# Regenerating a one-core hybrid decoder in the order its own list schedule found, with PSUM banks dealt again in eleven rounds

## The chip, the cores and the metric

The kernel runs on one core of a Trainium2 chip, as one launch. The metric is the device time of one execution in microseconds (us). The time before is the median of three runs.

## The reference, cut to what matters

One layer of a decoder trunk over 4096 tokens of width 1024: a norm, one wide input projection, two groups of recurrent heads that read it, an output projection with a residual add, and a last norm.

```python
h = _rmsnorm(x, norm_w)
u = (h @ w_in).astype(f32)
...
q_in = qc * jnp.exp(b)                    # gated linear attention, 4 heads, in chunks
k_in = kc * jnp.exp(-b)
...
def step(S, inp):                          # RWKV-7, 8 heads of 64, one token after another
    r_t, w_t, k_t, v_t, kk_t, a_t = inp
    sa = jnp.einsum('bhvk,bhk->bhv', S, -kk_t)
    S = (S * w_t[:, :, None, :]
         + sa[..., None] * (kk_t * a_t)[:, :, None, :]
         + v_t[..., None] * k_t[:, :, None, :])
    y = jnp.einsum('bhvk,bhk->bhv', S, r_t)
    return S, y
...
merged = jnp.concatenate([gla_out, rwkv_out], axis=-1).astype(x.dtype)
return x + merged @ w_out
```

## The kernel before

**Tiling.** The tokens are cut into 8 blocks of 512. A weight or an activation is held as two fp16 halves, so a projection of 128 columns is 3 x 8 pairs of matmuls with 512 moving columns. A pair is two matmuls of 64 columns each that run beside each other in the array (`duo`, L497, whose inner matmul stands on L509; all other instructions stand on L457, where the recording engine puts them). A block has 17 projections for the RWKV group (tiles `wr`), 12 for the attention group (`wg`; four of them, the values, are written with the operands exchanged and stand as `bank<-wg,x` with 128 moving columns, 384 matmuls for each two), and 8 for the output (`wo`).

**The recurrence.** A unit is a pair of RWKV heads of a block, so there are 32 units, numbered 0 to 31. `rwkv_ab` (L899) makes its operands: after the projections of key and receptance DVE writes `DD` and `bk`, PE multiplies them (`bank<-DD,bk`, 16 matmuls), and the masked product `Nb` has to be inverted. The inversion goes through DRAM (`nd`, then the tile `f`), runs as 62 small dependent steps on POOL (tiles `Tc`, `tm`; on DVE for unit 31 alone), goes back through DRAM (`td`), and ends in `rwkv_i` (L1049) with `bank<-Ta,Nb` and `bank<-Nb,Ta` on PE. `rwkv_c` (L1071) then runs the chain of 8 chunks: `ch<-sv,DD` on PE, a copy `us` on ACT, `ch<-us,Nb` on PE, a copy `uv` on ACT, `ch<-uv,bk` on PE, and the new state `sv` on DVE, three matmul steps for a chunk, each waiting for the one ahead of it. The chains of the units follow each other, since the state tile of a head pair goes from block to block. `rwkv_d` (L1114) normalises the outcome (`bank<-crs,bones`).

**The end.** `out_last` (L1339) makes the last block's output in two parts: the six mixing tiles that are ready early (`bank<-x,wo`), and then the tiles of units 30 and 31 (`bank<-x,x`, 96 matmuls), a norm and the stores.

**The start.** `stream_w` (L1463) reads, scales and splits all 37 weight tiles during the first block, on ACT and DVE.

**What sets the order.** Nothing is issued as the Python runs. Generators (`stream_x` to `stream_o`, and the chains) are advanced by `run` (L477), which keeps a rough clock with `account` (L183) and takes the ready generator of least priority. Each operation is recorded by `put` (L240) as a `Step` with its engine, a modelled duration, and the steps it must follow, found from the regions of tiles that it reads and writes (`parts`, L117; `whole`, L217). Some decisions are taken in this recording and never again: which of the six PSUM banks (`bank0` to `bank5`) a result gets (`need`, L789, takes the one that the rough clock says is free first), and so which earlier reader it has to wait for. Columns of small tables (`TABLES`, L100: scales, packed parameters, carries) are no regions for `parts`; `whole` lists them, and a step that shares only such a column with an earlier one follows its start, without a duration.

Then a list schedule is made. `forward` (L281) places the steps in time on six engines with a priority for each; `backward` (L349) makes the next priorities from the end times. Ten passes of both are made from the first order for each of five settings (`keep`, the bonus for staying in the same shape of array, and `look`, how far ahead an engine waits for a better step), the order with the smallest modelled end is kept, and the instructions are written in order of their modelled start times:

```python
first_order = forward([s.t0 for s in steps])
best = first_order
for keep, look in ((0.5, 0.15), (0.5, 0.3), (0.7, 0.3), (1.0, 0.15), (2.0, 0.3)):
    start, end = first_order
    for _ in range(10):
        start, end = forward(backward(end), keep, look)
        best = min(best, (start, end), key=lambda x: max(x[1]))
```

Every engine and the one DMA queue, SP's, then works through its instructions in that order.

Of the kernel before, what the change touches and what calls it, by code (L numbers as in the profile page):

```python
# [20 lines left out]
P = 128  # L21
DM = 1024
# [24 lines left out]
NC = TB // C  # L47
GUP = 2.0 ** 19
# [33 lines left out]
def hymba_kernel(ctx, tc, xT, wt, wg, wo, wua, gup, pk, ck, out):  # L82
# [16 lines left out]
    TABLES = ("pkt", "scl", "invs", "hinv", "mu_s", "omu_s", "carry", "wosc", "woinv", "gnh", "lnh")  # L99
    FINE = {"Nb": 32, "f": 16}  # L100
    HEADS, XS = set(), set()
    now = [0.0]
    streams = []
    ready, used, busy = {}, {}, {}

    def dram(ap):

        name = ap.tensor.name
        if name.startswith("nd"):
            return [(name, i) for i in (range(4) if ap.shape[0] == 32 and len(ap.shape) == 2 else [ap.offset // (NC * 1024) % 4])]  # L110
        if name.startswith("td"):
            return [(name, i) for i in (range(4) if ap.ap[0][0] >= 1024 else [ap.offset // 1024 % 4])]
        if name.startswith("wdr"):
            return [(name, i) for i in ([ap.offset // (P * DM) % 2] if ap.ap[0][1] == P and len(ap.shape) == 3 and ap.shape[1] == KT and ap.shape[2] == P else range(2))]
        return [(name, 0)]

    def parts(ap):  # L117
        if ap.tensor.name == out.tensor.name or ap.tensor.name.rsplit("_", 1)[0] in TABLES:
            return []
        if ap.space == DRAM:  # L120
            return dram(ap)
        a = ap.start_partition()
        tag = ap.tensor.name.rsplit("_", 1)[0].rstrip("0123456789_")
        if tag in FINE:
            q = FINE[tag]
            return [(ap.tensor.name, h) for h in range(a // q, (a + ap.shape[0] - 1) // q + 1)]
        hs = range(a // 64, (a + ap.shape[0] - 1) // 64 + 1)
        if ap.tensor.name in HEADS:
            o = ap.offset % P // 64
            e = range(2) if ap.ap[-1][1] > 64 else range(o, o + 1)  # L130
            return [(ap.tensor.name, h, i) for h in hs for i in e]
        if ap.tensor.name in XS:
            o = ap.offset % (4 * TB) // TB
            e = range(o, o + max(1, math.prod(ap.shape[1:]) // TB)) if ap.dtype == F16 else range(4)
            return [(ap.tensor.name, h, 2 + i) for h in hs for i in e]
        return [(ap.tensor.name, h) for h in hs]

    def place(eng, t, d):

        q = busy.setdefault(eng, [])  # L140
        while q and q[0][1] < now[0] - 100:
            q.pop(0)
        i = 0
        for i, (a, e) in enumerate(q):
            if t + d <= a:
                break
            t = max(t, e)
        else:
            i = len(q)
        q.insert(i, (t, t + d))  # L150
        return t

    class Array:


        def __init__(self):
            self.tile, self.form, self.f32, self.free, self.clock = {}, None, False, 0.0, [0, 0.0, True]

        def put(self, t, d, cols, tiles):
            r, c, f32 = tiles[:3]  # L160
            form = (r[1] - r[0], c[1] - c[0]) + tuple(tiles[3:])
            q = [(i, j) for i in range(r[0], r[1]) for j in range(c[0], c[1])]
            turn = form != self.form
            t = max([t, self.free] + [self.tile.get(k, 0.0) for k in (self.tile if turn else q)]) + 0.09 * turn
            w, k = int(t / 3.413), self.clock
            if w > k[0]:
                k[:] = [w, 0.0, w == k[0] + 1 and k[1] >= 3060]
            k[1] += cols
            d *= 1 if k[2] else 2
            full = len(q) == 16  # L170
            if full and f32 == 2:
                d += 0.005
            elif f32 and form == (2, 4):
                d += 0.008
            for k in q:
                self.tile[k] = t + (d if full or not f32 else 0.66 * d)
            self.form, self.f32 = form, f32 > 0
            self.free = t + (d if full or turn and f32 else d / 2 if f32 and form != (4, 1) else 0.014)
            return t, d

    array = Array()

    def account(eng, out, ins, d, lag, cols=0, tiles=None):  # L183
        rdy = lambda k: (lambda r: r[0] + early(r[1], eng))(ready.get(k, (0.0, "")))
        t = max([0.0] + [rdy(k) for a in ins for k in parts(a)]
                + [used.get(k, 0.0) for k in parts(out)]
                + [rdy(k) for k in parts(out) if eng != "T"])
        if eng == "T":
            t0, d = array.put(max(t, now[0]), d, cols, tiles)
            t, now[0] = t0, array.free  # L190
        else:
            if eng == "D":
                t0 = place("H", t, 0.5)
                t = t0 + 1.15
            t = place(eng, t, d)
            if eng != "D":
                t0 = t
        for a in ins:
            for k in parts(a):
                used[k] = max(used.get(k, 0.0), t + d + (0.95 if eng == "D" else 0.1))  # L200
        for k in parts(out):
            ready[k] = (t + d + lag, eng)
        return t0

    def early(a, b):

        if a not in "VSGT" or b not in "VSGT" or not a:
            return 0.0
        if a == b:
            return {"V": -0.075, "S": -0.1, "G": -0.18, "T": 0.0}[a]  # L210
        return -0.045 if a == "T" else 0.0 if b == "T" else -0.04

    table = [0]
    steps, wkey, rkey, wlast, readers = [], {}, {}, {}, {}
    last, turn, lead = [None, 0], [0], []

    def whole(ap):  # L217
        if ap.tensor.name == out.tensor.name:
            return []
        if ap.space == DRAM:  # L220
            return dram(ap)
        if ap.tensor.name.rsplit("_", 1)[0] in TABLES:
            w = math.prod(ap.tensor.shape[1:])
            return [(ap.tensor.name, i) for i in range(ap.offset % w, ap.offset % w + math.prod(ap.shape[1:]))]
        return parts(ap)

    class Step:


        def __init__(self, n, t0, eng, d, lag, cols, tiles, tab, f, both=False):  # L230
            self.n, self.t0, self.eng, self.d, self.lag, self.f, self.both = n, t0, eng, d, lag, f, both
            self.cols, self.tiles, self.tab, self.on, self.to, self.next = cols, tiles, tab, {}, [], None
            self.form = tiles and (tiles[0][1] - tiles[0][0], tiles[1][1] - tiles[1][0]) + tuple(tiles[3:])
# [6 lines left out]
    def put(t0, eng, d, lag, cols, tiles, tab, outs, ins, f):  # L240
# [3 lines left out]
        for k in list(ki) + list(ko):  # L244
            t0 = max(t0, wkey.get(k, 0.0))
# [1372 lines left out]
```

## Time and profile before

| | |
|---|---|
| median of three runs | 2261.45 us (2260.09 to 2263.47) |
| the profiled execution, own time | 2259.63 us |
| its span, first to last instruction | 2257.9 us |
| granted clock of TensorE, mean | 0.985 |
| DVE busy | 1706.8 us, 76% |
| ACT busy | 1249.7 us, 55% |
| POOL busy | 874.7 us, 39% |

A row of a timeline gives the start and the length in us, the engine, the line, the operation, what is written and read, the shape, the type and the count, and in brackets the idle time of the engine ahead of it with what ended it. PEld is the loading of weights on PE. A float32 matmul stands as two in the trace. In a table of windows the columns are the stretch, its length, the busy time and the number of instructions of PE, PEld, DVE, ACT and POOL, the granted clock of TensorE, the share of the DMA engines and their rate.

### The profile page before, as it was taken

The numbers are of one execution on the slowest core, as the hardware profiler recorded it, in microseconds if no ns is written. First come the engines' busy times: TensorE is split into PE (matmuls) and PEld (weight loads), VectorE is DVE, ScalarE is ACT, GpSimd is POOL, SyncE is SP. The second block draws the span as 40 slices with busy tenths as digits, with TensorE's granted clock in tenths as the row PEclk, the third lists the DMA queues.
The fourth block names the chain that finished last, engine by engine and source line by source line (L and its number), as shares of the span: only waits on it lengthen the run. The fifth ranks groups of instructions, "written<-read, shape, count | busy, mean of one in ns | idle before, by whom it ended". The sixth has DMA issues, their size and how long they took to land.

```text
span 2257.9 us, 75272 instructions
## 1 busy us (share of the span) xinstructions
PE 2154.3 (95%) x30800; PEld 1377.6 (61%) x30800; DVE 1706.8 (76%) x3801; ACT 1249.7 (55%) x3229; POOL 874.7 (39%) x2212
## 2 busy tenths in 40 slices
PE   7899999989999999999999999999999999999986
PEld 3656665556755567556675666655675565756653
DVE  7989788488783887768776886847878578776866
ACT  7677674455554646545554547445565555545442
POOL 2551334425344342436525154342624444262400
PEclk9999999999999999999999999999999999999988
DMA  6786554465344553456434553445534455344432
GB/s 193 223 262 207 166 181 146 114 194 145 88 127 127 185 149 94 116 150 202 120 103 126 179 156 110 116 129 178 156 92 123 140 179 149 100 118 137 146 86 80
DMA packets 275455, 326.91 MB, mean 145 GB/s; under 512 B 131572, under 2 KB 132772, under 8 KB 275108
## 3 DMA queue, kind: packets, MB, share of 16 engines
q1 hardware_dynamic: 275108, 322.10, 48.7%
q8 instruction: 241, 3.95, 0.7%
q14 instruction: 106, 0.87, 0.1%
HBM read 276.94 MB, written 45.05 MB: 143 GB/s over the span
## 4 chain that ended last, share of the span: by engine, by line
PE 63%; DVE 21%; DMA 8%; ACT 3%; issue 3%; SPq 1%; POOL 0%; DVEq 0%; ACTq 0%; POOLq 0%
PE bank L509 50%; PE bank L457 8%; PE ch L509 4%; DMA xr<-in_xT_dram 3%; DVE DD L457 3%; DVE nta L457 2%; DVE bk L457 2%; PE y L457 1%; DVE x L457 1%; SPq L457 1%; DVE xr L457 1%; DVE sv L457 1%; DVE Nb L457 1%; PE y L509 1%; DVE mgr L457 1%
## 5 line engine op out<-in xcount | busy, mean ns | idle before, releaser
L509 PE MATMUL bank<-x,wr 128*64 128x512 f16 x6528 | 795.5, 381 | 10.4 <-DVE DD L457 5.4
L457 POOL TENSOR_TENSOR tm<-Tc,f 128x60 f32<-128x60 f32 (+24 forms) x961 | 350.0, 364 | 667.7 <-DMA f<-nd 585.4
L509 PEld LDWEIGHTS <-wr 128*64 128x64 f16 x6528 | 361.1, 110 | 265.0 <-issue 27.2
L457 POOL TENSOR_TENSOR Tc<-Tc,tm 128x60 f32<-128x60 f32 (+24 forms) x961 | 357.3, 372 | 74.4
L509 PE MATMUL bank<-x,wg 128*64 128x512 f16 x3072 | 373.1, 384 | 3.8 <-ACT ta L457 2.2
L509 PE MATMUL bank<-x,wo 128*64 128x512 f16 x2976 | 360.9, 383 | 3.4 <-DVE DD L457 2.8
L457 POOL TENSOR_TENSOR xacc<-xacc,xr 128x512 f32<-128x512 f32 x98 | 129.7, 1324 | 364.0 <-ACT xr L457 235.2
L509 PEld LDWEIGHTS <-wg 128*64 128x64 f16 x3072 | 172.3, 111 | 130.5 <-issue 9.9
L457 DVE SCALAR_TENSOR_TENSOR sv<-ch,PC,psd 64x64 f32<-64x64 f32 x448 | 126.3, 282 | 143.3 <-PE ch L509 129.6
L509 PEld LDWEIGHTS <-wo 128*64 128x64 f16 x2976 | 162.8, 111 | 115.9 <-issue 9.2
L509 PEld LDWEIGHTS <-x 128*64 128x64 f16 x6240 | 190.8, 111 | 30.1 <-issue 20.0
L509 PE MATMUL bank<-wg,x 128*64 128x128 f16 x6144 | 194.8, 220 | 11.4 <-DMA wg<-wdr 7.2
L457 ACT ACTIVATE psd<-sv,PC 128x128 f32<-128x128 f32 x256 | 102.3, 400 | 165.3 <-DVE sv L457 143.0
L457 ACT COPY us<-ch 64x64 f32<-64x64 f32 x512 | 104.7, 205 | 94.5 <-PE ch L509 86.4
L457 ACT COPY uv<-ch 64x64 f32<-64x64 f32 x512 | 105.0, 205 | 93.9 <-PE ch L509 88.6
L457 ACT ACTIVATE sa<-bank,mu_s 128x512 f32<-128x512 f32 x104 | 71.5, 688 | 73.2 <-PE bank L509 69.9
L457 DVE COPY_PREDICATED Nb<-mc,bank 64x512 f32<-64x512 uint8 x128 | 92.8, 727 | 8.4 <-PE bank L457 6.4
L509 PEld LDWEIGHTS ch<-us,Nb 128*64 128x64 f32 x1024 | 68.5, 138 | 48.5 <-ACT us L457 15.3
L509 PEld LDWEIGHTS ch<-uv,bk 128*64 128x64 f32 x1024 | 68.0, 139 | 47.5 <-ACT uv L457 12.8
L509 PEld LDWEIGHTS ch<-sv,DD 128*64 128x64 f32 x1024 | 67.0, 138 | 46.7 <-DVE sv L457 14.4
L457 DVE COPY_PREDICATED DD<-mc,bank 64x512 f32<-64x512 uint8 x128 | 93.4, 731 | 2.3
L457 PE MATMUL bank<-DD,bk 64*128 64x128 f32 x1024 | 77.7, 286 | 11.4 <-DVE bk L457 7.4
(333 smaller groups left out, 3559.8 us busy)
## 6 DMA issues: line engine op xcount, KB each, us to landing
wr<-wdr SPq DMA_DIRECT2D x256, 256.0 KB
wg<-wdr SPq DMA_DIRECT2D x184, 256.0 KB
xr<-in_xT_dram SPq DMA_DIRECT2D x176, 256.0 KB
wo<-wdr SPq DMA_DIRECT2D x128, 256.0 KB
f<-nd SPq DMA_DIRECT2D x128, 128.0 KB
x<-in_wt_dram SPq DMA_DIRECT2D x29, 512.0 KB
wdr<-wo SPq DMA_DIRECT2D x25, 512.0 KB
out_dram<-mgg SPq DMA_DIRECT2D x33, 256.0 KB
```

The lines of the kernel that those rows point to most:

```text
L457: put(t0, self.name, d, lag, cols, tiles, tab, outs, ins, lambda: f(*a, **kw))
L509: nc.tensor.matmul(x, lhsT=l, rhs=y, start=start, stop=stop)
```

## The change

The recording is wrapped into a function `build(guide)`, and everything in it moves one level to the right. It is called eleven times. The first time `guide` is empty and the recording goes as before. In each later round `guide` holds, for every step of the round ahead (by the name of its generator and its number in it), the start and the end that the list schedule gave it:

- `run` advances the generator whose next step is due first by `guide`, in place of the one of least priority.
- `need` sorts the banks by the time at which they are left by `guide`, and if the bank it would take is left more than 1 us after the asking generator's next step is due, it puts the generator off once until then.
- `put` takes the start in `guide` as the step's first rank.

In each round there are five passes of `forward` and `backward` with one setting, `keep` 1.0 and `look` 0.15; the round with the smallest modelled end of the eleven is the one that is written out. Tiles are made once and shared by the rounds (`store`). Columns of tables become regions of `parts`; `whole` goes, and all dependencies carry their latency. The diff is shown without the changes of indentation and cut to its core; `forward`, `backward`, `account`'s body and the streams are as they were.

```diff
+LOOKS = ((1.0, 0.15),)
+PASSES = 5
+PUT_OFF = 1.0
+ROUNDS = (LOOKS,) * 11
...
+    store = {}
+    ident = one.tile([P, P], F32, tag="ident_0", name="ident_0")
+    make_identity(nc, ident)
+
+    def build(guide):
...
+        cur, nth, leave = ["init"], {}, {}
+        due = lambda who: guide.get((who, nth.get(who, 0)), (-1.0, -1.0))
...
-        if ap.tensor.name == out.tensor.name or ap.tensor.name.rsplit("_", 1)[0] in TABLES:
+            if ap.tensor.name == out.tensor.name:
             return []
...
+            if tag in TABLES:
+                w = math.prod(ap.tensor.shape[1:])
+                return [(ap.tensor.name, i) for i in range(ap.offset % w, ap.offset % w + math.prod(ap.shape[1:]))]
...
-        keys = lambda aps: {k: k in {y for x in aps for y in parts(x)} for a in aps for k in whole(a)}
+            keys = lambda aps: dict.fromkeys(k for a in aps for k in parts(a))
...
+            key = (cur[0], nth.get(cur[0], 0))
+            nth[cur[0]] = key[1] + 1
+            if key in guide:
+                t0 = guide[key][0]
+                for a in outs + ins:
+                    if a.space == PSUM:
+                        leave[a.tensor.name] = max(leave.get(a.tensor.name, 0.0), guide[key][1])
...
             can = [s for s in streams if s[2] is None or s[2]()]
+                if guide:
+                    s = min(can, key=lambda s: max(s[1], due(s[4])[0]))
+                else:
...
-            banks.sort(key=bank_free)
-            if len(banks) >= n and bank_free(banks[n - 1]) <= now[0]:
+                banks.sort(key=(lambda t: leave.get(t.tensor.name, 0.0)) if guide else bank_free)
+                if len(banks) >= n and (guide or bank_free(banks[n - 1]) <= now[0]):
+                    t = leave.get(banks[n - 1].tensor.name, 0.0)
+                    if guide and not put_off and t > due(cur[0])[0] + PUT_OFF:
+                        put_off = True
+                        yield (t,)
+                        continue
                 break
...
+        guide, best = {}, None
+        for looks in ROUNDS:
+            steps, forward, backward = build(guide)
         first_order = forward([s.t0 for s in steps])
-        best = first_order
-        for keep, look in ((0.5, 0.15), (0.5, 0.3), (0.7, 0.3), (1.0, 0.15), (2.0, 0.3)):
+            mine = first_order
+            for keep, look in looks:
             start, end = first_order
-            for _ in range(10):
+                for _ in range(PASSES):
                 start, end = forward(backward(end), keep, look)
-                best = min(best, (start, end), key=lambda x: max(x[1]))
-        start, end = best
+                    mine = min(mine, (start, end), key=lambda x: max(x[1]))
+            if best is None or max(mine[1]) < max(best[2]):
+                best = (steps,) + mine
+            guide = {s.key: (mine[0][s.n], mine[1][s.n]) for s in steps}
+        steps, start, end = best
```

**What moves on the engines.** The number of matmuls is the same, 25288 instructions, and so are the lists of DVE, ACT and POOL but for their order. The names end in buffer numbers that the two programs count differently (`DD_0_131` and `DD_0_132` before are `DD_0_133` and `DD_0_134` now; `wo_138` is `wo_140`). PE changes the shape of its tiles 698 times before and 666 times now.

The first place is on PE, at the last of the 16 products `bank<-DD,bk` of unit 31, behind which its inversion starts. Before:

```order
L457 MATMUL bank_0_187<-DD_0_132,bk_242 128x128
L457 MATMUL bank_0_185<-DD_0_132,bk_242 128x128
L509 LDWEIGHTS wg_232
L509 MATMUL bank_0_182<-x_1_0_0_80,wg_232 64x512
L509 LDWEIGHTS wg_232
L509 MATMUL bank_0_182<-x_1_0_0_80,wg_232 64x512
```

And now:

```order
L472 MATMUL bank_0_188<-DD_0_134,bk_242 128x128
L472 MATMUL bank_0_184<-DD_0_134,bk_242 128x128
L531 LDWEIGHTS x_1_0_0_87
L531 MATMUL bank_0_186<-wg_231,x_1_0_0_87 64x128
L531 LDWEIGHTS x_1_0_0_87
L531 MATMUL bank_0_186<-wg_231,x_1_0_0_87 64x128
```

The last value projections of the attention group (`bank<-wg,x`, 384 matmuls) stood ahead of unit 31's products and now stand behind them. From these products to the unit's `bank<-Ta,Nb` there are 364 matmuls before, none of them `bank<-wg,x`, and 788 now, 384 of them `bank<-wg,x`; those with 512 moving columns are 248 before and 262 now.

The second place is on PE too, further on, in the chain of unit 30 (`ch`), while unit 31's inversion runs. Before:

```order
L457 MATMUL bank_0_187<-r_199,bones_98 32x128 x4
L509 MATMUL ch_262<-sv_254,DD_0_131 64x64 x2
L509 MATMUL ch_262<-us_263,Nb_0_134 64x64 x2
L509 MATMUL ch_262<-uv_133,bk_241 64x64 x2
L509 MATMUL ch_262<-sv_254,DD_0_131 64x64 x2
L457 MATMUL bank_0_187<-ident_102,v_200 128x128 x4
L509 MATMUL ch_262<-us_263,Nb_0_134 64x64 x2
L509 MATMUL ch_262<-uv_133,bk_241 64x64 x2
L509 MATMUL ch_262<-sv_254,DD_0_131 64x64 x2
L509 MATMUL bank_0_182<-ident_102,amo_281 64x128 x2
L509 MATMUL ch_262<-us_263,Nb_0_134 64x64 x2
L509 MATMUL ch_262<-uv_133,bk_241 64x64 x2
```

And now, from the same reduction of `r`:

```order
L472 MATMUL bank_0_185<-r_199,bones_105 32x128 x4
L531 LDWEIGHTS wo_140
L531 MATMUL bank_0_188<-x_0_0_0_83,wo_140 64x512
L531 LDWEIGHTS wo_140
L531 MATMUL bank_0_188<-x_0_0_0_83,wo_140 64x512
L531 MATMUL ch_262<-sv_254,DD_0_133 64x64 x2
L531 LDWEIGHTS wo_140
L531 MATMUL bank_0_188<-x_0_0_0_83,wo_140 64x512
L531 LDWEIGHTS wo_140
L531 MATMUL bank_0_188<-x_0_0_0_83,wo_140 64x512
L531 LDWEIGHTS wo_140
L531 MATMUL bank_0_188<-x_0_1_0_84,wo_140 64x512
```

Nine steps of the chain followed each other with two small products with the identity between them; now matmuls of the output projection and of the last projection of the RWKV group stand between the steps. In the whole program 15 steps of the chains had at most two matmuls between them and the next, now 7 have.

The third place is on DVE in the first block, where it writes `DD` and `bk` of unit 1 among the splits of weights (`wo<-x,scl,wo`, `wr<-x,scl,wr`). Before:

```order
L457 SCALAR_TENSOR_TENSOR wo_138<-x_1_0_0_80,scl_178,wo_138 128x1024
L457 SCALAR_TENSOR_TENSOR rn_195<-rk_194,pkt_95,rn_195 128x512
L457 SCALAR_TENSOR_TENSOR ta_197<-ta_197,rn_195 128x512
L457 SCALAR_TENSOR_TENSOR r_199<-bank_0_182,omu_s_119,sa_216 128x512
L457 SCALAR_TENSOR_TENSOR bk_242<-ta_197,E_196 64x8x64
L457 TENSOR_TENSOR DD_0_132<-r_199,EP_233 64x8x64 x2
L457 TENSOR_SCALAR scl_178<-pw_205 128x1
L457 TENSOR_TENSOR DD_0_132<-rn_195,EP_233 64x8x64 x2
```

And now:

```order
L472 SCALAR_TENSOR_TENSOR r_199<-bank_0_185,omu_s_121,sa_216 128x512
L472 TENSOR_SCALAR pw_205<-amW_210 128x1
L472 TENSOR_TENSOR DD_0_134<-r_199,EP_233 64x8x64
L472 TENSOR_SCALAR pw_205<-pw_205 128x1
L472 SCALAR_TENSOR_TENSOR wr_214<-x_1_3_0_90,scl_180,wr_213 128x1024
L472 TENSOR_SCALAR scl_180<-pw_205 128x1
L472 TENSOR_TENSOR DD_0_134<-r_199,EP_233 64x8x64
```

The receptance `r` is taken from its bank, and the first half of `DD` written, ahead of a split of weights and of `rn`, where both followed them. On PE 98 matmuls stand between the end of that projection and the first `bank<-DD,bk` of unit 1 before, and 246 now.

More of the change, by code (lines that the diff above doesn't have):

```diff
@@ L94, in hymba_kernel @@
     psp = ctx.enter_context(tc.tile_pool(name="psp", bufs=1, space=PSUM))
[L99 to L115, printed above, removed]
@@ L117, in parts @@
-    def parts(ap):
-        if ap.tensor.name == out.tensor.name or ap.tensor.name.rsplit("_", 1)[0] in TABLES:
[L119 to L233, printed above, removed]
-        def follow(self, m, lat):
-            if m is not self:
-                o = self.on.get(m)
-                self.on[m] = lat if o is None else max(o, -1.0 if lat is None else lat)
@@ L1538, in hymba_kernel @@
-    with tc.manual_schedule(engines={getattr(mybir.EngineType, e) for e in ("PE", "DVE", "Activation", "Pool", "SP")}):
+            yield from halves(range(K0), 0)
+            iv = sb(rt, [P, 3, KT], F32, "ivl")
+            V.tensor_scalar_mul(iv[:, 0], woinv, am[:, 1:2])
+            part = mgt[:K0] + [mfree["g"].pop(0), mfree["r"].pop(0)]
+            for n in range(KT):
+                w = yield from get_w(NWT + n, "o")
+                for i in range(2):
+                    D.dma_start(ws[i][:, n], wdr[NWT + n].rearrange("a p k t -> p a k t")[:, :, K0 + i, :])
+                ps = yield from proj(w, mh, "o", K0)
+                xr = sb(rt, [P, TB], F32, "xr", NXR)
+                D.dma_start(xr, xT[P * n:P * n + P, TB * b:TB * b + TB])
+                V.scalar_tensor_tensor(part[n], ps, iv[:, 0, n:n + 1], xr, ALU.mult, ALU.add)
@@ new lines, in out_last @@
+            rs = newton(pst[:, 0:P], 1.0 / DM, 1e-6, None, "g")
+            pb = yield from need("o")
+            yield after(rs)
+            spread(rs, pb, 1)
+            for n in range(KT):
+                V.scalar_tensor_tensor(part[n], part[n], pkt[:, PK_FN + n:PK_FN + n + 1], pb, ALU.mult, ALU.mult)
+                D.dma_start(out[P * n:P * n + P, TB * b:TB * b + TB], part[n])
+            if not guide:
+                yield now[0]
+        done = dict.fromkeys(("A", "C", "G", "GE", "GV", "GG", "GH", "I", "IS", "CC", "O", "X", "W", "SU", "N"), 0)
@@ new lines, in stream_x, with stream_a @@
+        def stream_x():
+            for b in range(NB):
+                yield lambda: done["O"] >= b - 1 and (b == 0 or done["A"] > 4 * b - 4 and done["W"] >= NWT)
+                yield from x_block(b)
+                done["X"] += 1
+        def stream_a():
+            for b in range(NB):
+                yield lambda: done["X"] > b
+                xs = x16[b % 2]
+                WA = shift((yield from proj((yield from get_w(W_WA, "r")), xs, "r")), 12, sb(rt, [P, TB], F32, "v"))
+                if not done["SU"]:
+                    yield lambda: done["SU"]
+                LR = yield from lora(WA)
+                for p in range(4):
+                    yield from rwkv_ab(4 * b + p, p, b, xs, LR)
```

2402 lines of the change are left out of this document (1245 added, 1157 removed).

## The prediction

> **What bounds the kernel now.** I read the shares of the engines first, then stretches of the span, then who PE waits for, and last the timeline where it waits.
>
> ```profile
> span 2257.9 us, 75272 instructions
> PE 2154.3 (95%) x30800; PEld 1377.6 (61%) x30800; DVE 1706.8 (76%) x3801; ACT 1249.7 (55%) x3229; POOL 874.7 (39%) x2212
> ```
>
> PE is busy for 2154.3 of 2257.9 us, so the order alone can win no more than the 104 us of its idle time and what PE loses at a lowered clock. The table of windows shows where that lies: the first block, the second, a block in the middle, the stretch of unit 31's inversion, and the end.
>
> ```profile
> 22.00:307.00 285.00, 263.06 (x3840) 173.24 (x3840) 247.19 (x648) 202.26 (x439) 103.10 (x233) 0.97 0.66 202
> 307.00:562.00 255.00, 238.71 (x3174) 147.87 (x3170) 197.32 (x425) 138.93 (x369) 106.70 (x276) 0.97 0.52 152
> 830.00:1096.00 266.00, 263.21 (x3833) 168.87 (x3831) 199.63 (x421) 145.98 (x390) 114.52 (x288) 1.00 0.48 139
> 2133.00:2182.00 49.00, 42.86 (x481) 25.87 (x482) 40.14 (x127) 22.16 (x62) 2.91 (x15) 0.90 0.33 80
> 2182.00:2258.00 76.00, 55.41 (x756) 33.95 (x752) 42.58 (x100) 24.14 (x73) 0.00 (x0) 0.88 0.28 88
> ```
>
> The middle block has 2.8 us of idle PE and the full clock: nothing is to be had there. The first two blocks have 21.9 and 16.3 us idle and a clock of 0.97, the last 125 us have 6.1 and 20.6 us idle and 0.90 and 0.88. So the gain lies at both ends. Who is waited for, on PE:
>
> ```profile
> PE ch L509 <- ACT us L457: 8.9, 7, 3.2
> PE bank L509 <- DMA wg<-wdr: 8.4, 7, 3.2
> PE bank L509 <- DVE DD L457: 8.4, 8, 2.8
> ```
>
> No single resource stands behind it: the chain's copy on ACT, a weight that lands late, a bank that DVE has not read yet, each with about 1.1 us a time. It is the order that decides, place by place.
>
> **The change part by part.** The matmuls are the same, so the sum has a term for each place where the new rows stand otherwise, one for the shape of the array, and one for waits that arise anew.
>
> *Term 1, the last inversion.* From unit 31's last product to its inverse:
>
> ```profile
> 2131.66 2.50 PE L457 MATMUL bank<-DD,bk 64*128 64x128 f32 x30
> 2157.65 1.27 PE L509 MATMUL bank<-x,wr 128*64 128x512 f16 x10
> 2160.12 0.60 PE L509 MATMUL bank<-x,wr 128*64 128x512 f16 x4
> 2160.65 0.43 PE L457 MATMUL bank<-r,bones 128*32 128x128 f32 x8
> 2161.05 0.34 PE L509 MATMUL ch<-sv,DD 128*64 128x64 f32 x4
> 2162.11 0.34 PE L509 MATMUL ch<-us,Nb 128*64 128x64 f32 x4 [0.72 <-ACT us L457]
> 2162.97 0.34 PE L509 MATMUL ch<-uv,bk 128*64 128x64 f32 x4 [0.52 <-ACT uv L457]
> 2164.37 0.34 PE L509 MATMUL ch<-sv,DD 128*64 128x64 f32 x4 [1.06 <-DVE sv L457]
> 2172.41 1.06 PE L509 MATMUL bank<-x,wo 128*64 128x512 f16 x4 [0.53 <-ACT x L457]
> 2173.43 2.90 PE L509 MATMUL bank<-x,wo 128*64 128x512 f16 x16
> 2176.99 0.89 DVE L457 STREAM_TRANSPOSE Ta<-Nb 32x256 f32<-32x256 f32 x2
> 2182.33 0.69 PE L457 MATMUL bank<-Ta,Nb 32*32 32x32 f32 x32
> ```
>
> The products end at 2134.2 and the inverse is back on DVE at 2177.9, so the way through DRAM and the 62 steps takes 43.7 us whatever PE does. In that time PE ran out of other work: from 2161.05 to 2172.41 it had the bare chain, with an idle stretch in nearly every step. By the order rows, 384 `bank<-wg,x` matmuls now stand in this window that stood ahead of it, and 14 more with 512 columns.
>
> ```profile
> L509 PE MATMUL bank<-x,wr 128*64 128x512 f16 x6528 | 795.5, 381 | 10.4 <-DVE DD L457 5.4 <-ACT x L457 2.1 <-DMA wr<-wdr 1.9
> L509 PE MATMUL bank<-wg,x 128*64 128x128 f16 x6144 | 194.8, 220 | 11.4 <-DMA wg<-wdr 7.2 <-issue 2.9 <-ACT Nb L457 1.4
> 2165.00:2176.00 11.00, 7.46 (x52) 4.82 (x54) 10.54 (x26) 8.05 (x24) 0.00 (x0) 0.53 0.37 77
> ```
>
> They cost 384 x 194.8/6144 = 12.2 us and 14 x 795.5/6528 = 1.7 us, 13.9 us together. The hole offers 49.00 - 42.86 = 6.1 us of idle time, and 49 x (1 - 0.90) = 4.9 us at the lowered clock, nearly all of it in the 11 us at 0.53 that the third row shows. So the window takes in 11 us of the 13.9 for nothing and grows by the other 3; the places that the matmuls leave shrink by all of it. Next late is the chain of unit 30 itself, which with five pairs to a step goes at PE's pace. The stretch behind the window has the same rows in nearly the same order (a unit's chain, then 96 `bank<-x,x`, a norm); I give it 1 us. **Term 1: -12 us.** Bounds: nothing, if the hole opens elsewhere in the same chain, and -17, if part of the 20.6 us behind it goes too.
>
> A rule bears on the 4.9 us. The Trainium skill, page "TensorE: Matmul & The Clock Gate", section "HAM oscillation — how this bites in real kernels", says that the array falls to half its clock after idle gaps of more than some 3.4 us. The trace differs: the longest wait quoted from this hole is 1.06 us, and the clock still fell to 0.53. By the page the drop would have another cause and filling the hole would not take it away, so that this term would be near -7 instead of -12 and the forecast about 2242; I go by the row.
>
> *Term 2, the first two blocks.*
>
> ```profile
> 106.69 0.74 DVE L457 SCALAR_TENSOR_TENSOR r<-bank,omu_s,sa 128x512 f32<-128x512 f32 x1
> 110.30 0.77 PE L457 MATMUL bank<-DD,bk 64*128 64x128 f32 x2 [3.15 <-DVE DD L457]
> 110.88 0.80 DVE L457 SCALAR_TENSOR_TENSOR bk<-ta,E 64x512 f32<-64x512 f32 x1
> 111.74 1.65 PE L457 MATMUL bank<-DD,bk 64*128 64x128 f32 x12 [0.67 <-DVE bk L457]
> 478.81 4.39 PE L509 MATMUL bank<-wg,x 128*64 128x128 f16 x92 [3.25 <-DMA wg<-wdr]
> ```
>
> Unit 1's products wait 3.15 and 0.67 us for DVE. Now 246 matmuls stand where 98 did, and DVE takes `r` earlier, so these 3.8 us should go. The wait of 3.25 us at 478.8 is for a weight whose load was issued late; the loads of that projection now stand further ahead of their use. With some of the lowered clock (3% of 540 us is 16 us in the two blocks) I take 3 us more. **Term 2: -10 us.** Bounds: nothing, because DVE is busy for 247.19 of 285 us in the first block and its list of instructions is the same, and what PE gains there may have to wait for DVE all the same; and -49, the whole excess over the middle block (19 + 14 us idle, and the 16 of clock). DVE's share there is the reason why I stay near the small end.
>
> *Term 3, unit 21.*
>
> ```profile
> 1554.56 0.69 PE L509 MATMUL bank<-wg,x 128*64 128x128 f16 x18 [1.92 <-issue]
> 1555.30 0.48 PE L457 MATMUL bank<-DD,bk 64*128 64x128 f32 x2
> 1558.19 0.48 PE L509 MATMUL ch<-us,Nb 128*64 128x64 f32 x4 [2.40 <-ACT us L457]
> 1558.95 1.49 PE L509 MATMUL bank<-x,wg 128*64 128x512 f16 x6 [0.28 <-DMA wg<-wdr]
> ```
>
> Here a late weight and a chain step with only one product ahead of it cost 1.92 + 2.40 + 0.28 = 4.6 us, and the six matmuls behind them run 1.49 us where they need 0.7. In the new order the step has 20 matmuls ahead of it. **Term 3: -5 us**, between nothing and -8.
>
> *Term 4, shapes.* Two pairs ahead of a product of another shape take 2160.65 - 2160.12 = 0.53 us, where the five ahead of a chain step in the same shape go at 0.22 each, 0.44 for two: 0.09 us a turn. 32 turns fewer: **-3 us**.
>
> *Term 5, new waits.* PE runs its rows in order, so a late row holds up all behind it, and DVE and ACT, which read PE's banks, with it. Unit 26's products now have 68 matmuls, some 4.4 us, between the end of the receptance projection and themselves, where DVE needs 5.0 us from `r` at 106.69 to the last `bk` at 111.68 and ACT's shift comes before it; unit 31's are short too. I take six waits of 1.05 us (8.4 us in 8 times is the mean for `DD`). **+6 us**, between 0 and +30, one in ten of the 296 projections waiting for a bank.
>
> The queue of SP has the same 1821 transfers; where one is moved past others I cost it at nothing, since PE's work of some microseconds stands ahead of most uses, and at 3.25 us, as at 478.8, where it does not. Regions for table columns add no instruction; they move small steps, and are costed at nothing beside the places above.
>
> The sum is -12 - 10 - 5 - 3 + 6 = -24 us. Against the profiled execution's own 2259.63 us (span 2257.9) that is 2235.6; the median of the runs shown, 2261.45, lies 1.8 above it, so **2237 us**.
>
> **The rivals.** *Banks in time for the plan, late on the chip (slower).* `need` may now take a bank that is left up to 1 us after its taker is due, where before it waited for one that its clock called free. If DVE and ACT run later than the plan by a little, each such take holds PE for about 1.05 us. Without term 5 the sum is -30; 29 late takes of 296 eat it, and one in seven, 42, gives 2261.45 - 30 + 44 = 2275. For it: PE already waits for `DD` and for ACT. Against it: these waits are 8.4 us in all now, and in the plan too every bank is waited for.
>
> *The hole moves (no change).* The 13.9 us of matmuls are taken from the time of unit 30's products, and if that inversion then runs short, the loss of term 1 comes back there and the small terms cancel: 2258. Against it: from unit 30's products to its inverse there are still 284 matmuls with 512 columns and 384 of the short ones.
>
> *Both ends close (faster yet).* If term 2 is 35 instead of 10, because every late start in the first 560 us goes: 2212. For it: 15 chain steps had next to nothing behind them, and 7 have now. Against it: DVE's 87% there.
>
> *The plan is the old one.* The eleven rounds might have kept the first, without dealing banks again. The order rows show other banks and other places, so this is out.
>
> **How the numbers follow.** The forecast has 0.68, both ends closing 0.15, the hole moving 0.09, late banks 0.08. The range goes from 2215, where term 1 is at -17 and term 2 near -20 with term 3 at its end, to 2257, where only the shapes are left: it leaves out the better half of the fast case, the slow one and half of the unchanged one. A measurement of this kernel tells 0.2%, 4.5 us, from no change: faster 0.83, within it 0.09, slower 0.08.
>
> **What would show it.** Term 1: no row between unit 31's products and its inverse in which two chain steps follow with idle time between them, and the clock near 1.00 there. Term 2: the first two blocks with less than 38 us of idle PE together. Term 3: no lowered clock near 1557. Term 5: waits of PE for `DD` above 8.4 us. It would be wrong if the middle blocks, at 2.8 us idle now, show 6 us or more each, or if the last 76 us grow.

## The result, and the profile after

| | before | after |
|---|---|---|
| median of four runs each | 2260.78 us (2260.09 to 2263.47) | 2224.26 us (2219.75 to 2227.11) |
| profiled execution, own time | 2259.63 us | 2225.85 us |
| its span | 2257.9 us | 2224.1 us |

The ratio is 0.9834, with a 95% interval from 0.9815 to 0.9854: 36.5 us less by the medians, 33.8 by the profiled executions. The forecast was 24 less. The head of the page after:

```profile
span 2224.1 us, 75265 instructions
PE 2139.1 (96%) x30800; PEld 1371.9 (62%) x30800; DVE 1712.6 (77%) x3801; ACT 1249.4 (56%) x3229; POOL 871.5 (39%) x2212
```

PE has the same 30800 rows. It is busy for 15.2 us less, and idle for 85.0 us where it was 103.6. The table of windows of after, for the first block, the second, the third, the sixth, the stretch from unit 31's products to the inverse's use, and the end (a stretch begins where the first `bank<-x,wr` of its block stands):

```profile
20.00:312.00 292.00, 271.30 (x3885) 174.78 (x3885) 249.89 (x660) 204.84 (x444) 106.95 (x239) 0.96 0.66 202
312.00:549.00 237.00, 227.43 (x3049) 140.57 (x3047) 192.55 (x412) 132.50 (x352) 106.78 (x259) 0.99 0.54 158
549.00:812.00 263.00, 259.03 (x3769) 167.82 (x3768) 196.83 (x409) 142.97 (x384) 108.90 (x282) 1.00 0.48 137
1345.00:1613.00 268.00, 262.98 (x3856) 169.28 (x3848) 199.29 (x422) 147.27 (x390) 108.25 (x281) 0.99 0.49 138
2097.00:2151.00 54.00, 54.00 (x918) 38.30 (x918) 46.98 (x140) 28.23 (x77) 3.67 (x18) 0.97 0.39 105
2151.00:2224.00 73.00, 54.32 (x748) 33.16 (x744) 43.26 (x100) 23.53 (x69) 0.00 (x0) 0.88 0.33 104
```

The stretch of the inversion has 918 rows of matmuls instead of 481 and no idle time at all; the second block is 18 us shorter. But the blocks don't hold the same work before and after, so lengths alone mislead. In the next table the work of a stretch's products is estimated and taken off its length: 0.449 ns for every column that PE moves, and 0.105 us for each turn of shape. The columns are counted from the instructions, with matmuls that run side by side taken as one, and with a float32 column taken as four: in the trace after, 8 pairs of `bank<-SC,vt` with 128 float32 columns take 1.91 us, 0.24 a pair, and 6 pairs of `bank<-x,wr` with 512 fp16 columns 1.46 us, also 0.24. Both figures are scaled so that the quiet middle blocks leave next to nothing. What remains is idle time and lowered clock beyond those of the quiet blocks, which have some 3 to 5 us of idle time each.

| stretch | before, us | after, us | difference |
|---|---|---|---|
| start | 17.6 | 15.9 | -1.7 |
| first block | 31.8 | 32.2 | +0.4 |
| second | 24.9 | 15.0 | -9.9 |
| third | 5.8 | -0.3 | -6.1 |
| fourth and fifth | 3.4 | 4.8 | +1.4 |
| sixth | 7.6 | 4.7 | -2.9 |
| seventh | 0.4 | 0.2 | -0.2 |
| eighth, to unit 31's products | 1.2 | 2.5 | +1.3 |
| inversion of unit 31 | 10.6 | 0.7 | -9.9 |
| end | 27.3 | 24.3 | -3.0 |

The differences sum to -30.6 us; the work itself is 3.4 us less, since in the traces the shape turns 665 times instead of 697. Both together are the 33.8 us of the spans, to a rounding. Who PE waits for, after (us in total, times, longest; four lines of the list):

```profile
PE ch L531 <- ACT us L472: 8.4, 11, 1.4
PE bank L472 <- DVE bk L472: 5.8, 8, 2.7
PE bank L531 <- ACT wo L472: 4.1, 5, 1.5
PE bank L531 <- DMA wg<-wdr: 2.9, 5, 0.8
```

The wait for `DD`, 8.4 us before, is gone from the list, and the one for the weights `wg` fell from 8.4 to 2.9. A longer wait (0.55 us before, 2.66 now) stands directly ahead of the stretch that was filled, as the timeline of PE after shows (start, length, instruction, and in brackets the idle time ahead of it):

```profile
2090.34 0.66 PE L472 MATMUL bank<-ident,v 128*128 128x128 f32 x4
2093.66 4.58 PE L472 MATMUL bank<-DD,bk 64*128 64x128 f32 x32 [2.66 <-DVE bk L472]
2098.17 7.38 PE L531 MATMUL bank<-wg,x 128*64 128x128 f16 x224
```

The projection that used to stand ahead of unit 31's products, and gave DVE time to write `bk`, now stands behind them.

### The profile page after: what moved, and what is told of

Same layout as the page of the kernel before. It is cut to its first block, busy times and chain, and to the rows that moved or that the text cites. A ratio compares the mean times of both kernels' runs of the same rounds, so it can differ in the third digit from the quotient of the medians.

```text
span 2224.1 us, 75265 instructions
## 1 busy us (share of the span) xinstructions
PE 2139.1 (96%) x30800; PEld 1371.9 (62%) x30800; DVE 1712.6 (77%) x3801; ACT 1249.4 (56%) x3229; POOL 871.5 (39%) x2212
## 4 chain that ended last, share of the span: by engine, by line
PE 61%; DVE 19%; DMA 10%; ACT 3%; issue 3%; SPq 2%; POOL 2%; DVEq 0%; ACTq 0%; POOLq 0%
PE bank L531 48%; PE bank L472 7%; PE ch L531 3%; DMA xr<-in_xT_dram 2%; DVE DD L472 2%; SPq L472 2%; DMA rn<-bcda 2%; DVE nta L472 2%; DVE bk L472 1%; DVE x L472 1%; PE y L472 1%; DMA wg<-wdr 1%; DMA bcda<-nya 1%; DVE Nb L472 1%; DVE xr L472 1%
## 5 line engine op out<-in xcount | busy, mean ns | idle before, releaser
L531 PE MATMUL bank<-x,wr 128*64 128x512 f16 x6528 | 807.7, 382 | 9.9 <-ACT Nb L472 2.3
L531 PEld LDWEIGHTS <-wr 128*64 128x64 f16 x6528 | 361.7, 110 | 259.8 <-issue 30.6
L472 POOL MEMSET Tc<- 32x8 f32 (+1 forms) x160 | 23.6, 148 | 189.2 <-DMA td<-Tc 175.0
```

The costliest lines, as they stand in the source:

```text
L472: put(t0, self.name, d, lag, cols, tiles, tab, outs, ins, lambda: f(*a, **kw))
L531: nc.tensor.matmul(x, lhsT=l, rhs=y, start=start, stop=stop)
```

## The experiments

### One move, done alone and taken back

The table above invites a simple story: the moved V projection is worth the 10 us of its stretch. Two kernels test it. `late_v` is the kernel before with that move alone:

```diff
+        if n == 2 * NB - 1:
+            yield lambda: gate          # filled by unit 31's last bank<-DD,bk
...
+                    held_v[0] = n == 2 * NB - 1
...
+        if held_v[0]:
+            s.follow(gate[0], None)
```

> The kernel before, with one thing of the change: the last of the V projections (384 products of `wg` with `x`) is recorded behind the last product of unit 31's `bank<-DD,bk`, so that 480 of these products stand behind it, as in the changed kernel, and not 80. All else is generated as before. Theory of places (the gain is the sum of a few stretches of the order, each worth what PE waited there): 10 to 13 us less than before, a ratio of 0.994 to 0.9956; in the trace the stretch between unit 31's products and its inverse's last use holds under 2 us of idle PE (6.1 before), and the first two blocks stay as before. Rival (the hole moves: the projection's products are missed where they are taken from): within 3 us of before, with new idle PE of 5 us or more in the last block ahead of unit 31's products. Rival (the clock follows from single long waits, of which this stretch has none): 6 to 8 us less.

Measured: 2261.95 us, a ratio of 1.001 (0.9995 to 1.0025). **Nothing is gained**, as the rival of the moving hole had it. The table of windows of `late_v`, for the last block up to unit 31's products, the inversion and the end:

```profile
1901.00:2130.00 229.00, 220.76 (x3027) 139.46 (x3028) 170.84 (x367) 125.11 (x347) 100.53 (x266) 0.99 0.43 123
2130.00:2177.00 47.00, 45.56 (x834) 32.89 (x832) 34.77 (x112) 18.42 (x53) 0.73 (x5) 0.99 0.36 90
2177.00:2255.00 78.00, 61.62 (x828) 37.85 (x824) 50.83 (x120) 30.38 (x86) 0.00 (x0) 0.93 0.33 102
```

The inversion is filled as expected: 834 rows, 1.4 us idle, a clock of 0.99. By the accounting above the last two stretches together leave 15.4 us less than before. The last block gives back 6.9 of it, nearly all in one place of PE's timeline of `late_v`:

```profile
2118.81 0.41 PE L512 MATMUL bank<-x,wg 128*64 128x512 f16 x2
2119.03 0.28 PE L512 MATMUL ch<-sv,DD 128*64 128x64 f32 x2
2120.25 0.33 PE L512 MATMUL ch<-sv,DD 128*64 128x64 f32 x2 [0.94 <-DVE sv L460]
2126.73 4.49 PE L460 MATMUL bank<-DD,bk 64*128 64x128 f32 x32 [6.16 <-DVE bk L460]
```

The projection had covered DVE's work on `bk`; with it gone, PE stands for 6.16 us ahead of the very products behind which it was put. The remainders of the other blocks grow by 4.8 us in sum (the first by 3.8, the seventh by 2.7), and I found no place in the trace that explains these (the list schedule is made anew for the whole program); the profiled span is 3.1 us below before's while the median is level.

`early_v` is the changed kernel with the move forbidden:

```diff
+            if u == 4 * NB - 1 and done["GV"] < 2 * NB:
+                yield lambda: done["GV"] == 2 * NB
...
+            if held_p[0] and eng == "T":
+                s.follow(gate[-1], None)   # unit 31's products behind the last V product
```

> The changed kernel, with that one thing taken back: unit 31's `bank<-DD,bk` is made to follow the last V projection, so that 110 of the `wg` products are left behind it instead of 480. The eleven rounds stand, and may fill the stretch with other work. Theory of places: 8 to 13 us more than the changed kernel's 2224.3, 2232 to 2237, a ratio to before of 0.988 to 0.990, with idle PE of 4 us or more back between unit 31's products and its inverse. Rival (the rounds find other fill, and what was gained is the rounds' general work): within 3 us of the changed kernel, ratio 0.983 to 0.985. Rival (the hole moves): faster than the changed kernel.

Measured: 2221.06 us, a ratio of 0.983 (0.981 to 0.985), the same as the changed kernel: the rival that the rounds find other fill came true. The table of windows of `early_v` for the same three stretches:

```profile
1866.00:2097.00 231.00, 227.72 (x3408) 147.41 (x3402) 171.09 (x360) 127.51 (x349) 101.59 (x264) 1.00 0.43 127
2097.00:2142.00 45.00, 42.89 (x546) 26.18 (x546) 40.33 (x133) 23.25 (x62) 2.29 (x12) 1.00 0.40 95
2142.00:2217.00 75.00, 55.85 (x761) 34.59 (x756) 44.07 (x104) 25.33 (x76) 0.00 (x0) 0.90 0.29 95
```

The stretch of the inversion has only 546 rows of matmuls, yet 2.1 us idle and the full clock (before: 481, 6.1 us, 0.90). The rounds spread what there is over the chain steps, five or six pairs to a step. Ahead of unit 31's products stand 160 `bank<-wg,x`, and these products wait for nothing. So the move is one of several ways to close the hole; neither it nor its absence decides the time.

### How many rounds

`one_round` and `one_round_search` cut the rounds to one:

```diff
-ROUNDS = (LOOKS,) * 11
+ROUNDS = (LOOKS,)
```

The second also has the search of the kernel before, five settings and ten passes.

> The changed kernel with ROUNDS cut to a single round: the program is generated, set in order once and put out in that order, with one setting and five passes; table columns stay regions of the order model, and banks are dealt by the order found once. Its `wg` products stand as before at the end (84 behind unit 31's last product), and tile shapes turn 677 times (697 before, 665 changed). Theory that the repeated rounds bring the gain: 0 to 12 us less than before (2249 to 2261; ratio 0.9947 to 1.000), with the idle PE of the last inversion as before. Rival (one setting and the table columns as regions bring it, and further rounds only shuffle): 25 us or more less than before, a ratio of 0.989 or lower.

> The changed kernel with one round, and with the five settings and ten passes of the kernel before: what is left of the change is the table columns as timed regions of the order model and the bank order of a single regeneration. Theory that repeated rounds bring the gain: within 6 us of before (ratio 0.997 to 1.003). Rival (the table columns, timed now, let the order avoid the waits of the first two blocks): 8 us or more less than before, with block 1's idle PE at 10 us or less (16.3 before).

Measured: `one_round` 2276.24 us, 1.0063 (1.0048 to 1.0078), slower than before and outside what either theory gave; `one_round_search` 2265.23 us, 1.0009 (0.9997 to 1.0021). So the new search by itself is worse than the old one by 11 us, and the table columns as regions bring nothing to a program that is recorded once. (Both expectations speak of banks dealt by the order found; with a single round `guide` is empty, so the banks are still taken by the rough clock, and the table columns are all that `one_round_search` has of the change.)

`rounds_2`, `rounds_4` and `rounds_22` change the number alone.

> The changed kernel with two rounds: one generation by due times and one by the order found, with its banks dealt anew; 88 of the `wg` products stand behind unit 31's last product, as before. Theory that the gain comes with the dealt banks and grows with the rounds, until the last inversion is filled too: between one round (ratio 1.006) and eleven (0.983), a ratio of 0.990 to 1.000, with 4 us or more of idle PE still in the last inversion. Rival (the first regeneration with dealt banks already brings it): 0.987 or lower. Rival (single orders scatter by 15 us either way, and the differences between these kernels are chance): 1.003 or higher.

> The changed kernel with four rounds; 480 of the `wg` products stand behind unit 31's last product, as with eleven. Theory that the gain grows over a few rounds and then settles: a ratio of 0.980 to 0.990, idle PE in the last inversion under 2 us. Rival (all eleven are needed): 0.992 or higher. Rival (chance): no order between two, four and eleven rounds.

> The changed kernel with twice as many rounds, 22. Theory that the rounds settle after a few and then only trade one order for another of the same kind: within 8 us of the changed kernel, a ratio to before of 0.980 to 0.987. Rival (each round takes out more waits): 8 us or more below it, a ratio under 0.980, with less idle PE than 70 us in all (76.3 changed, 94.8 before).

| rounds | median, us | ratio to before (95%) | idle ahead of matmuls, us |
|---|---|---|---|
| 1 | 2276.24 | 1.0063 (1.0048 to 1.0078) | 102.5 |
| 2 | 2274.32 | 1.0057 (1.0039 to 1.0074) | 108.7 |
| 4 | 2247.38 | 0.9943 (0.9927 to 0.9959) | 93.8 |
| 11 | 2224.26 | 0.9834 (0.9815 to 0.9854) | 76.3 |
| 22 | 2217.08 | 0.9799 (0.9778 to 0.9820) | 73.8 |

Before the change the last column is 94.8 us. Both `rounds_2` and `rounds_4` came out slower than my theory's ranges, on the side of the rivals: two rounds bring nothing, and four not half, so the gain needs more rounds than I thought. Chance, the third rival, doesn't explain the whole row, since the time falls beyond the intervals from two rounds to four and from four to eleven, and three kernels of eleven rounds (the changed one, `early_v` and, below, `no_put_off`) lie within 3.2 us of each other. Four rounds are the telling case. The stretch of the inversion is already filled there, and the kernel is still 23 us slower than with eleven. The table of windows of `rounds_4`, for the second block, the last and the inversion:

```profile
315.00:561.00 246.00, 228.99 (x3089) 145.37 (x3087) 192.35 (x414) 131.19 (x352) 102.67 (x261) 0.97 0.53 155
1890.00:2114.00 224.00, 217.41 (x3004) 138.12 (x3002) 165.15 (x350) 123.42 (x342) 95.98 (x252) 0.99 0.44 125
2114.00:2167.00 53.00, 52.38 (x924) 37.58 (x920) 43.26 (x139) 25.28 (x70) 4.79 (x21) 0.99 0.35 91
```

The second block has 17.0 us idle, as before the change, and the last block 6.6, with a wait of 4.47 us for `bk` ahead of unit 31's products, by the timeline of PE of `rounds_4`:

```profile
2111.22 4.01 PE L472 MATMUL bank<-DD,bk 64*128 64x128 f32 x32 [4.47 <-DVE bk L472]
```

Twenty-two rounds gave the fastest kernel of all, 2217.08 us; against eleven its interval overlaps by 0.0005, so that step is likely but not shown, and it lies on the border between the theory and the rival of `rounds_22`.

One more rival is that each round is a draw, and that more rounds only give more draws to choose from. The modelled ends of the rounds speak against it; the list schedule computes them from the kernel's source alone, so they are no measurement. In the changed kernel they are 2223.0, 2208.0, 2184.9, 2174.8 and 2163.8 us for the first five rounds, so they fall step by step; from the ninth, 2153.8, to the twenty-second they go to and fro between 2153.6 and 2163.6. With four rounds the fourth is written out, with eleven the ninth, with twenty-two the sixteenth, and the last two are 0.2 us apart in the model. The kernel before has a modelled end of 2205.5: the model promised 52 us, and 36.5 were measured.

### What the rounds need

`no_deal` and `no_deal_22` leave out the dealing of the banks, `no_put_off` only the putting off, and `tables_untimed` and `tables_untimed_22` the time of the table columns:

```diff
-PUT_OFF = 1.0
+PUT_OFF = 1e9
...
-                banks.sort(key=(lambda t: leave.get(t.tensor.name, 0.0)) if guide else bank_free)
+                if not guide:
+                    banks.sort(key=bank_free)
```

The edit of the two `tables_untimed` kernels puts `whole` and the dependencies without a duration back as they were before the change. That generators are taken by due time, and that steps are ranked by `guide`, was not left out by itself.

> The changed kernel with eleven rounds, but the banks are not dealt by the times at which their products leave in the order found: each is given out in the order in which it came back, and nothing is put off for want of a bank. Theory that the gain comes from regenerating the program in the order found (each ring of buffers is then given out in that order, and the next schedule is freer): at most 8 us above the changed kernel's 2224.3, a ratio to before of 0.980 to 0.987, with idle PE of block 1 below 12 us and of the last inversion below 3 us. Rival (the deal of the banks brings it): 15 us or more above the changed kernel, a ratio of 0.990 or higher, with waits of `bank` products for the reader of their bank (`bk`, `rk`) of more than 10 us together.

> Twenty-two rounds, with each bank given out in the order in which it came back and nothing put off: the pair of the 22-round kernel (ratio 0.980) as the eleven-round kernel without the deal (0.998) is of the changed kernel (0.983). Theory that the deal of the banks carries the gain: 0.990 or higher again, with more idle PE than 85 us in all (73.8 with the deal). Rival (the eleven-round kernel without the deal was one bad order): 0.986 or lower.

> The changed kernel with the banks dealt by the order found, but a step is taken whenever a bank is free at all (PUT_OFF so large that it never acts). Theory that regenerating brings the gain: ratio to before 0.980 to 0.987. Rival (waiting for the right bank is what keeps the order found): a ratio of 0.990 or higher.

> The changed kernel with eleven rounds, but the table columns order the work as in the kernel before, without a time of their own in the model. Theory that regenerating brings the gain: ratio to before 0.980 to 0.988, with block 1 near the changed kernel's 237 us. Rival (the regions of the tables keep the first blocks' waits away): block 1 stays at 250 us or more (256 before), and the ratio is 0.990 or higher.

> Twenty-two rounds with the table columns ordering the work but without a time of their own, as in the kernel before. Theory that timing the table columns carries a part: 0.985 to 0.992 again (0.989 with eleven rounds), against 0.980 with the regions timed. Rival (chance): 0.983 or lower.

| left out | 11 rounds, us and ratio (95%) | 22 rounds, us and ratio (95%) |
|---|---|---|
| nothing | 2224.26, 0.9834 (0.9815 to 0.9854) | 2217.08, 0.9799 (0.9778 to 0.9820) |
| the deal, and the putting off | 2256.17, 0.9979 (0.9963 to 0.9995) | 2250.68, 0.9955 (0.9940 to 0.9970) |
| the putting off alone | 2223.24, 0.9830 (0.9810 to 0.9849) | - |
| the time of table columns | 2237.92, 0.9889 (0.9869 to 0.9910) | 2239.64, 0.9905 (0.9887 to 0.9923) |

Without the deal the rounds bring 6 and 11 us, and with it 37 and 45; the difference is 32 us with eleven rounds and 34 with twenty-two, so it is not one bad order, and the rival of `no_deal`, that the deal brings the gain, came true. The modelled ends point the same way: without the deal they stay between 2171.7 and 2187.5 us from the eighth round to the twenty-second.

`no_deal` also shows once more that places don't add up. Here are its second block, its seventh and its inversion of unit 31 in the table of windows:

```profile
319.00:554.00 235.00, 224.80 (x3067) 144.00 (x3065) 189.36 (x406) 130.23 (x352) 101.71 (x251) 0.99 0.54 159
1622.00:1896.00 274.00, 266.53 (x3798) 171.34 (x3796) 200.14 (x423) 146.07 (x385) 99.91 (x265) 0.98 0.46 133
2125.00:2182.00 57.00, 55.31 (x912) 39.43 (x910) 44.47 (x134) 24.12 (x65) 2.98 (x15) 0.96 0.42 111
```

The second block and the inversion, both priced in the forecast, are closed nearly as well as in the changed kernel, with 10.2 and 1.7 us idle. Yet the profiled span is 2259.4 us, no shorter than before (the median is 6 us less): other blocks lost what these two gained, the seventh with 7.5 us idle for one, against 2.6 before.

The putting off does nothing. The time of the table columns is worth 14 and 23 us. My expectation that the second block (block 1 in its words) would show the tables' share was wrong: it is 240 us long there, near the changed kernel's 237, and the ratio with eleven rounds lies between what the theory and the rival gave. By the accounting of the stretches most is lost in the first block, 9 us with eleven rounds and 20 with twenty-two. That the tables bring nothing in one round and this much in eleven says that they help the rounds, not a single list schedule.

How the deal works was only read from waits. The three largest groups in `no_deal`'s list of PE's waits (us in total, times, longest):

```profile
PE bank L472 <- DVE bk L472: 13.5, 12, 5.6
PE bank L531 <- ACT wo L472: 13.1, 7, 2.9
PE bank L531 <- DMA wg<-wdr: 10.2, 12, 2.6
```

My expectation took `bk` for a bank's reader. It is an operand of the product that waits; `wo` is a bank's reader (PE waits to write a bank that ACT has not copied yet). I sorted all of PE's waits over 50 ns in this way: one for a tile that the product reads is for an operand, one for any other tile is for the bank.

| kernel | for operands, us | for banks, us |
|---|---|---|
| before | 71.4 | 19.9 |
| 11 rounds | 52.2 | 21.1 |
| 22 rounds | 49.3 | 21.6 |
| 11 rounds, no deal | 65.4 | 31.3 |
| 22 rounds, no deal | 61.6 | 26.9 |
| 4 rounds | 77.0 | 14.4 |

PE waits no less for banks than before. The 19 us that it saves are operands that come in time; without the deal the waits for banks grow by 5 to 10 us and those for operands by 12 to 13. Differences of a few us in the second column tell little: `no_put_off`, as fast as the changed kernel, has 24.6 there. The rest fits an order that is free to put work where an operand is late as long as a bank can be had for it. The order of cause is argued, not shown.

## Why the prediction was right, and where it was not

The time lies in the range and on the forecast side, 12.7 us below the value. By the steps of the sum:

- **Term 1, the last inversion, -12.** In the trace the sum came as sized: the stretch left 9.9 us less and the end 3.0, the last block 1.3 more, together -11.6. PE has no idle time there, and the clock is 0.97. The 43.7 us that the way through DRAM was to take "whatever PE does" did not hold: after, the products end at 2098.2 us and the inverse is on DVE at 2148.1, 49.8 us later, so the window grew by 5 us and not by 3. The timeline of DVE after:

```profile
2147.18 0.90 DVE L472 STREAM_TRANSPOSE Ta<-Nb 32x256 f32<-32x256 f32 x2 [0.70 <-DMA Nb<-td]
```

  And the experiments take away the meaning that the term gave it. The move alone is worth nothing, and forbidding it costs nothing. The step "the places that the matmuls leave shrink by all of it" is what failed in `late_v`: one of these places was the cover of `bk`, and it opened by 6.16 us. The rival of the moving hole looked for the loss at unit 30's inversion, and it was ahead of unit 31's products.
- **Term 2, the first two blocks, -10.** The sum is right (+0.4 and -9.9). The first block gained nothing, and DVE is busy there for 249.89 of 292 us, which was the reason for the lower bound; that DVE is what holds it was not tested, and `rounds_22` speaks against it: there the first block is 7 us shorter than after (the row is of its table of windows) with DVE as busy.

```profile
20.00:305.00 285.00, 267.36 (x3896) 172.80 (x3896) 250.07 (x660) 206.39 (x448) 114.72 (x257) 0.99 0.67 208
```

  The second gave all of it, with the wait for `wg` gone. Together they show 30.3 us idle, under the 38 named as the test.
- **Term 3, unit 21, -5.** Measured -2.9 for the block. What the prediction took for a late weight is a wait "for the issue", for which the profile names no releaser; it moved rather than went. The timeline of PE after:

```profile
1550.36 0.36 PE L531 MATMUL bank<-wg,x 128*64 128x128 f16 x6 [2.14 <-issue]
1550.52 1.86 PE L531 MATMUL bank<-x,wr 128*64 128x512 f16 x8
1557.44 1.27 PE L531 MATMUL bank<-x,wr 128*64 128x512 f16 x10
```

  And the table of windows of after there, with the clock as the third figure from the end:

```profile
1550.00:1556.00 6.00, 5.64 (x68) 3.85 (x69) 0.57 (x2) 2.26 (x6) 3.39 (x11) 0.72 0.58 180
```

  A wait of 2.14 us for the issue is left, and eight matmuls behind it take 1.86 us where ten take 1.27 a little later, at a clock of 0.72. The test "no lowered clock near 1557" was therefore met at 1557 and missed at 1551.
- **Term 4, shapes, -3.** 32 turns fewer; by the accounting 3.4 us of work. It was not tested by itself.
- **Term 5, new waits, +6: mis-sized.** The waits for `DD` that it was measured by vanished instead of growing, and unit 26's products wait for nothing. Of the six only one was found, the 2.66 us of unit 31, which is for an operand. The sum of PE's waits for banks is level, 19.9 and 21.1 us. With that difference, +1, as the term the forecast would have been 2232.
- **Not in the sum: the third block, -6.1.** Its row in the table of windows of before, which the prediction does not use, has 8 us idle, as against 2.8 in the fourth:

```profile
562.00:829.00 267.00, 259.02 (x3774) 168.78 (x3774) 198.07 (x417) 140.97 (x379) 108.23 (x275) 1.00 0.47 138
```

  After, it is 263 us with 4.0 idle. The statement that the gain lies at both ends was too narrow; the start, 1.7 us less, is not in the sum either.
- **The clock.** The rule of the Trainium skill that was weighed against term 1 (page "TensorE: Matmul & The Clock Gate", section "HAM oscillation — how this bites in real kernels") would have left the clock in the stretch where it was, as no single wait there was as long as its 3.4 us. The runs speak against it: in `late_v` and after, the clock of the stretch rose from 0.90 to 0.99 and 0.97 when the many short waits were filled, and a wait of 2.14 us goes with 0.72 above.

So the forecast of the sum was better than its picture of causes, and that terms 1 and 2 came out near their sizes is in part luck: the inversion is filled in `late_v` and `no_deal` too, in `no_deal` the second block as well, and the one gained nothing and the other 6 us. It priced places where the order was bad and took each to be won by the rows that now stand there. The runs show that the places are coupled, and that the gain belongs to the repeated recording with the banks dealt anew and the tables timed. Why the deal frees the order stays argued.

## What to carry to other kernels

A decision taken while recording (which buffer, which bank) binds every schedule made afterwards; record again in the order found, deal the buffers by that order, and repeat while the time falls; here four rounds were too few, and whether twenty-two are better than eleven is not shown. Before a product is moved to fill a hole, ask what it covers where it stands: the move alone brought about as much idle time ahead of the products as it took away behind them. When a trace shows a gain at one place, do that one thing alone before you call it the cause.

## What was not expected of the hardware

The clock falls after little idle time. Before the change it was 0.53 over 11 us in a stretch of the chain whose longest wait is 1.16 us; after, a wait of 2.66 us ahead of unit 31's products goes with 0.53 over the 7 us around their start, 6.31 us of them busy. The length of one wait does not decide it: in the same trace a wait of 2.09 us at 55.8 us leaves the clock at 1.00, where one of 2.14 us at 1550.4 goes with 0.72. A row of the timeline of before, one of after, and two of the table of windows of after:

```profile
2169.06 0.48 PE L509 MATMUL ch<-sv,DD 128*64 128x64 f32 x4 [1.16 <-DVE sv L457]
55.77 1.92 PE L531 MATMUL bank<-x,wg 128*64 128x512 f16 x16 [2.09 <-ACT wg L472]
55.00:62.00 7.00, 5.81 (x56) 3.12 (x56) 6.64 (x12) 6.68 (x14) 1.28 (x1) 1.00 0.57 158
2093.00:2100.00 7.00, 6.31 (x68) 5.82 (x70) 6.39 (x10) 0.40 (x1) 5.56 (x19) 0.53 0.01 2
```

So a wait can cost its own length and that of slow matmuls behind it: 6.31 busy us at 0.53 are some 3.0 us of lost work, an estimate from the last row. What decides whether the clock falls stays open.
